# Four more up-projection chunks a layer by seven products, with weight buffers of 4 KB made further ahead

## The chip, the cores and the metric

The kernel runs on one core of one Trainium2 chip. The metric is the device time of one execution in microseconds (us), and lower is better. TensorE (PE) multiplies, VectorE (DVE) and ScalarE (ACT) do the elementwise work, GpSimd (POOL) issues the accumulating DMAs and a few small operations, and SyncE (SP) issues the loads. PEld is TensorE's loading of stationary operands, which overlaps its multiplying.

## What is computed

An encoder of two residual layers over 512 tokens of 1024 features, in float32. Layer 0 mixes tokens by a gated linear attention (GLA) in two directions, layer 1 by grouped-query softmax attention. Each layer ends with a gated MLP whose up-projection gives 2 x 2816 features, a value half and a gate half:

```python
def conv_ffn(h, w_up, w_conv, b_conv, w_down):
    u = h @ w_up
    u = lax.conv_general_dilated(
        u, w_conv[:, None, :], window_strides=(1,), padding=[(1, 1)],
        dimension_numbers=('NWC', 'WIO', 'NWC'), feature_group_count=u.shape[-1]) + b_conv
    val, gate = jnp.split(u, 2, axis=-1)
    return (jax.nn.silu(gate) * val) @ w_down
...
for i in range(DEPTH):
    h = rmsnorm(x, norm_mix[i])
    ...
    x = x + conv_ffn(rmsnorm(x, norm_ffn[i]), ffn_w_up[i], ffn_w_conv[i],
                     ffn_b_conv[i], ffn_w_down[i])
```

## The kernel before

**Layout and precision.** Activations lie with features on the 128 partitions and the 512 tokens along the free axis; x is eight tiles of 128x512. Every float32 operand of a large product is split into a high part (rounded to fp32r by ACT) and a low part (the rest, by DVE), and a product is three matmuls: high x high, high x low, low x high (mm3, L359 to L363).

**Order of the program.** GLA, MLP of layer 0, attention, MLP of layer 1. The build puts the instructions of each engine into one fixed order, which need not be that of the source; an engine runs its own in that order.

**Weights.** The class Weights (L115 to L221) keeps a list `todo` of pieces in the order of use. Weights come in strips of 1 MB (8 KB a partition); a plain strip has two pieces of 4 KB. make() (L129) loads a strip into one of two `raw` buffers of 8 KB and splits a piece into `wh` (L204, ACT) and `wl` (L205, DVE), with three buffers of 4 KB for each. Some strips named in `by_dma` are split without DVE: ACT writes the high part (L144) and the negated high part (L145), and an accumulating DMA that POOL issues (L194, in flush()) adds the raw weights to the latter. piece() hands out a piece and makes others until `ahead` of them are ready: one ahead for plain pieces, three for those of a seven-product strip.

**The MLP** (ffn, L774) has 22 chunks of 128 value and 128 gate features. A plain chunk (plain_up, L785) is two tiles `up` of 128x512 with 24 matmuls each; DVE multiplies each by the tokens' factors (L803). A chunk named in SEVEN (seven_up, L824) is computed by a seven-product scheme on 2x2 blocks, as Strassen's: features in pairs of 128, tokens in two halves of 256. Its inputs are combined once a layer, during chunks 0 to 3 (prepare_input, L899). Its weights are four quarters a21, a11, a12, a22, from which summed() (L151) makes four pieces: h=0 holds a21+a11 and a11, h=1 a21+a22 and a11+a21+a22 (into the 8 KB tile `ring`), h=2 a12 and a22 (low part by DMA), h=3 the sum for product 3 (in `sq` tiles). Each product is 12 matmuls of 128x256 (L815). Results grow in PSUM banks r1 to r5 (tags acc with three banks, s and pt with two each); ACT copies partial results between banks (L831, L835, and L846, L847, L850 at the end), DVE combines them (L840, L848 to L854). The first product of a chunk is started within the chunk before it (begin_up).

After either form, act_up (L857) does the convolution (ACT L864, DVE L865 and L866), silu (L868) and the gate (L869); after each second chunk prepare() (L878) makes the combined operands of the down-projection (L875, L876 and small ones). After chunks 9 and 17, down_part (L921) does four strips of the down-projection by the same seven products, ACT copying at L935, L944 and L950, DVE adding into x (L951, L958 to L962). The last six chunks' part of the down-projection is plain (48 units of three matmuls, `dn`), the first 16 of which need only chunks 16 to 19.

Before the change SEVEN holds chunks 5, 11, 14, 18, 19 and 21, so a layer has 16 plain chunks, 6 by seven products, and 8 strips of the down-projection by seven products. The products of a chunk run in the order 1, 6, 7, 2, 5, [1 of the next], 4, 3, and those of a down strip likewise.

The tile `ring` is also used in GLA for the split values (values, L636) and in attention for copies of the probabilities.

Of the kernel before, what the change touches and what calls it, by code (L numbers as in the profile page):

```python
# [14 lines left out]
P = 128  # L15
# [33 lines left out]
SEVEN = (5, 11, 14, 18, 19, 21)  # L49
# [10 lines left out]
def hybrid_encoder_kernel(  # L60
# [54 lines left out]
    class Weights:  # L115
# [3 lines left out]
        def __init__(self):  # L119
            self.todo, self.made, self.raw, self.by_dma, self.pending = [], {}, {}, [], []  # L120
            self.sums, self.last, self.fine = set(), None, []

        def add(self, src, strips=None, pieces=2):
            for i in strips or range(src.shape[0]):
                self.todo += [(src, i, h) for h in range(pieces)]
                if pieces > 2:
                    self.sums.add((id(src), i))

        def make(self, key):  # L129
            src, i, h = key  # L130
            if h == 0 and (id(src), i) not in self.raw:
                t = sp.tile([P, 4 * S], F32, tag="raw", bufs=2, name=nm("raw"))
                n = 4 if any(src is a and i < m for a, m in self.fine) else 1
                for q in range(n):
                    sl = slice(q * 4 * S // n, (q + 1) * 4 * S // n)
                    sync.dma_start(t[:, sl], src[i, :, sl])
                self.raw[id(src), i] = t
            if (id(src), i) in self.sums:
                self.made[id(src), i, h] = self.summed(self.raw[id(src), i], h)
                return  # L140
            r = self.raw[id(src), i][:, h * 2 * S : (h + 1) * 2 * S]
            hi, lo = pair("wh", 3, F32R, "wh"), pair("wl", 3, F32R, "wl")
            if any(src is a and i < n for a, n in self.by_dma):
                act.activation(hi, r, AF.Copy)  # L144
                act.activation(lo, r, AF.Copy, scale=-1.0)  # L145
                self.pending.append((lo, r))
# [4 lines left out]
        def summed(self, raw, h):  # L151


            a21, a11, a12, a22 = (raw[:, n * S : (n + 1) * S] for n in range(4))
            if h == 0:
                r = tmp("t", "sum")
                with tc.issue_after(self.last.ins) if self.last else ExitStack():
                    dve.tensor_tensor(r, a21, a11, ALU.add)
                    dve.tensor_tensor(a21, a21, a22, ALU.add)
                hi, lo = pair("wh", 3, F32R, "wh"), pair("wl", 3, F32R, "wl")  # L160
                for sl, y in ((slice(0, S), r), (slice(S, 2 * S), a11)):
                    act.activation(hi[:, sl], y, AF.Copy)
                    dve.tensor_tensor(lo[:, sl], y, hi[:, sl].bitcast(F32), ALU.subtract)
                return hi, lo
            if h == 1:
                dve.tensor_tensor(a11, a21, a11, ALU.add)
                r = raw[:, : 2 * S]
            elif h == 2:
                r = raw[:, 2 * S :]
            else:  # L170
                r = tmp("sq", "sum4")
                dve.tensor_tensor(r, a11, a12, ALU.add)
                hi, lo = (sp.tile([P, S], F32R, tag="sq", bufs=3, name=nm(n)) for n in ("wh4", "wl4"))
                act.activation(hi, r, AF.Copy)
                self.last = dve.tensor_tensor(lo, r, hi.bitcast(F32), ALU.subtract)
                return hi, lo
            if h == 1:
                t = sp.tile([P, 4 * S], F32R, tag="ring", bufs=1, name=nm("ring"))
                hi, lo = t[:, : 2 * S], t[:, 2 * S :]
            else:  # L180
                hi, lo = pair("wh", 3, F32R, "wh"), pair("wl", 3, F32R, "wl")
            if h == 2:
                act.activation(hi, r, AF.Copy)
                act.activation(lo, r, AF.Copy, scale=-1.0)
                self.pending.append((lo, r))
            else:
                act.activation(hi, r, AF.Copy)
                dve.tensor_tensor(lo, r, hi.bitcast(F32), ALU.subtract)
# [8 lines left out]
        def split(self, hi, lo, r, pieces, first):  # L197
# [20 lines left out]
        def ahead(self, n):  # L218
            while self.todo and n > 0:
                self.make(self.todo.pop(0))  # L220
                n -= 1  # L221

# [28 lines left out]
    W.by_dma += [(a, 1) for a in qk_order + [w_av]] + [(w_aout, 2)]  # L251
# [6 lines left out]
    raw = [sp.tile([P, 4 * S], F32, tag="raw", bufs=2, name=f"first{i}") for i in range(2)]  # L258
    for c in range(KC):
        r = slice((c % 4) * S, (c % 4 + 1) * S)  # L260
        sync.dma_start(x[c], xT[c * P : (c + 1) * P, :])
        sync.dma_start(raw[c // 4][:, r], w_vg[c // 4, :, r])
        W.raw[id(w_vg), c // 4] = raw[c // 4]
# [175 lines left out]
    def gla(norm, nxt):  # L439
# [39 lines left out]
        rw = pair("wh", 3, F32R, "rw")  # L479
# [4 lines left out]
        graw = sp.tile([P, 4 * S], F32, tag="raw", bufs=2, name="graw")  # L484
        for i in range(4):
            sync.dma_start(graw[i * 32 : (i + 1) * 32, : 2 * S], w_gate)
        gst = big(F32R, "gst")
        act.activation(gst, graw[:, : 2 * S], AF.Copy)
        pool.tensor_tensor(gst[64:96, :], graw[64:96, : 2 * S], gst[64:96, :].bitcast(F32), ALU.subtract)
# [146 lines left out]
        def values(h):  # L636

            t = sp.tile([P, 4 * S], F32R, tag="ring", bufs=1, name=nm("vr"))
            for s in range(NT):
                r = v[s][:, h * DV : (h + 1) * DV]  # L640
                hi = t[:, s * DV : (s + 1) * DV]
                act.activation(hi, r, AF.Copy)
                dve.tensor_tensor(t[:, 2 * S + s * DV : 2 * S + (s + 1) * DV], r, hi.bitcast(F32), ALU.subtract)
            return [(t[:, s * DV : (s + 1) * DV], t[:, 2 * S + s * DV : 2 * S + (s + 1) * DV]) for s in range(NT)]
# [129 lines left out]
    def ffn(layer, norm, cw, nxt):  # L774
# [10 lines left out]
        def plain_up(m):  # L785

            pss = []
            for t in range(2):
                ps = bank("s" if t else "acc", "up")
                feature_tile(*W.half(up[layer], 2 * m + t, ahead.get((m, t), 1)), norm.hl, ps)  # L790
# [10 lines left out]
            for ps in pss:  # L801
                u = tmp("u", "u")
                dve.tensor_tensor(u, ps, norm.R, ALU.mult)  # L803
                yield u
# [19 lines left out]
        def seven_up(m):  # L824
# [28 lines left out]
            yield c  # L853
            dve.scalar_tensor_tensor(d, d, -1.0, norm.R, ALU.mult, ALU.mult)  # L854
            yield d

        def act_up(m):  # L857

            res = []
            for t, u in enumerate(begun.pop(0) if m in SEVEN else plain_up(m)):  # L860
# [6 lines left out]
                res.append(y)  # L867
# [53 lines left out]
        def down_part(part, m):  # L921
# [17 lines left out]
            for n in range(NQ):  # L939
# [7 lines left out]
                go(n, 2, r1, False)  # L947
# [3 lines left out]
                dve.tensor_tensor(c[:, :H], c[:, :H], r1, ALU.add)  # L951
                go(n, 4, r3, False)
                if n + 1 < NQ:
                    begin(n + 1)
                else:
                    begin_up(m + 1)
# [5 lines left out]
                dve.tensor_tensor(c[:, H:], c[:, H:], r2, ALU.add)  # L962

# [43 lines left out]
    def attention(norm, nxt):  # L1007
# [159 lines left out]
        ring = sp.tile([P, 4 * S], F32R, tag="ring", bufs=1, name=nm("ring"))  # L1167

        def copy(h, j):

            n = (h * NT + j) % 6
            if n < 4:
                t = ring[:, n * S : (n + 1) * S]
# [158 lines left out]
```

## Time and profile before

| what | value |
|---|---|
| median of 3 runs | 1104.43 us (1104.32 to 1105.28) |
| profiled execution | 1103.4 us, its span from first to last instruction; no other time of it is listed |
| PE / PEld / DVE / ACT / POOL busy | 1096.4 / 960.6 / 870.1 / 633.5 / 97.9 us |
| matmuls | 6212 |
| GLA, 0 to 225.7 us | 225.7 us |
| MLP of layer 0, to 574.7 us | 349.0 us |
| attention, to 749.8 us | 175.1 us |
| MLP of layer 1, to the end | 353.6 us |

Stage borders are read from the first `up` matmul of each layer and the last `dn` matmul of layer 0. A busy PE is not PE at its peak: a matmul's record runs from issue to drain, and its successors are issued meanwhile. What a matmul costs in a dense stretch is the distance between two starts, and that is read from the chain of work or the timeline. The same holds in a small way on DVE and ACT, where an instruction starts before the one ahead of it has quite ended.

### The profile page before, as it was taken

To read this page: it belongs to the slowest core of one execution; us is meant where nothing else is said; L and a number is where in the kernel's file an instruction comes from. 1 tells how busy PE (TensorE), PEld (TensorE's weight loads), DVE (VectorE), ACT (ScalarE), POOL (GpSimd) and SP (SyncE) were. 2 spreads that over 40 slices of the span, in tenths; PEclk is the share of its full clock that TensorE was granted. 3 is DMA by queue.
4 is the path that set the end of the run, shared out by engine and by line. 5 is a ranking of instruction groups with operands and counts; after the bars stand their busy time and mean duration, and the time that the engine had idled before them with its cause. 6 is when DMAs were issued, how large, how long until landed. Compare 5 with 4: busy or idle time off the path is not lost.

```text
span 1103.4 us, 16108 instructions
## 1 busy us (share of the span) xinstructions
PE 1096.4 (99%) x6212; PEld 960.6 (87%) x6212; DVE 870.1 (79%) x1441; ACT 633.5 (57%) x1034; POOL 97.9 (9%) x106
## 2 busy tenths in 40 slices
PE   9999999999999999999999999999999999999998
PEld 7888888888889988899888888788888998889987
DVE  6785775669998789987964578766999878997893
ACT  5565343446656556666664777645665655665660
POOL 0100222000000000000004343000000000000000
PEclk9999999999999999999999999999999999999999
DMA  6322222222516434364457765422151643445542
GB/s 232 134 96 89 79 100 77 77 77 80 169 45 175 129 98 140 124 173 115 140 152 182 181 178 152 163 77 81 72 166 50 167 134 97 138 129 143 145 134 77
DMA packets 33149, 136.91 MB, mean 124 GB/s; under 512 B 4016, under 2 KB 4528, under 8 KB 22704
## 3 DMA queue, kind: packets, MB, share of 16 engines
q1 hardware_dynamic: 21072, 102.16, 27.1%
q0 software_dynamic: 7104, 25.17, 11.6%
q10 hardware_dynamic: 4896, 8.55, 2.1%
q8 instruction: 49, 0.80, 0.3%
q14 instruction: 28, 0.23, 0.1%
HBM read 100.21 MB, written 2.10 MB: 93 GB/s over the span
## 4 chain that ended last, share of the span: by engine, by line
PE 92%; DVE 4%; DMA 2%; ACT 1%; issue 0%; POOL 0%; ACTq 0%; DVEq 0%; SPq 0%
PE r L815 24%; PE up L361 10%; PE up L362 10%; PE up L363 10%; PE vg L393 8%; PE op L419 8%; PE dn L363 2%; PE dn L361 2%; PE dn L362 2%; PE o L687 1%; DMA ring<-p 1%; PE av L393 1%; PE pt L1191 1%; PE A L361 1%; PE q L361 1%; PE in L620 1%
## 5 line engine op out<-in xcount | busy, mean ns | idle before, releaser
L361 PE MATMUL up<-xhl,wh 128*128 128x512 f32 x512 | 199.9, 390 | 0.0
L362 PE MATMUL up<-xhl,wh 128*128 128x512 f32 x512 | 199.5, 390 | 0.0
L363 PE MATMUL up<-xhl,wl 128*128 128x512 f32 x512 | 199.3, 389 | 0.0
L204 ACT ACTIVATE wh<-raw 128x1024 fp32r<-128x1024 f32 x108 | 114.1, 1057 | 128.8 <-PE up L362 34.0
L205 DVE TENSOR_TENSOR wl<-raw,wh 128x1024 fp32r<-128x1024 f32 x108 | 132.0, 1223 | 30.2 <-ACT wh L204 29.8
L815 PE MATMUL r<-gu,wh 128*128 128x256 f32 x640 | 116.6, 283 | 0.3 <-ACT r L950 0.3
L363 PEld LDWEIGHTS up<-xhl,wl 128*128 128x128 f32 x512 | 96.1, 188 | 20.2
L362 PEld LDWEIGHTS up<-xhl,wh 128*128 128x128 f32 x512 | 96.2, 188 | 19.2
L361 PEld LDWEIGHTS up<-xhl,wh 128*128 128x128 f32 x512 | 96.2, 188 | 19.2
L815 PEld LDWEIGHTS r<-gu,wh 128*128 128x128 f32 x640 | 99.7, 191 | 0.8 <-ACT r L950 0.5
L194 POOL DMA_DIRECT2D wl<-raw x44 | 38.9, 883 | 675.5 <-ACT r L935 195.3
L864 ACT ACTIVATE y<-u,cw 128x512 f32<-128x512 f32 x88 | 68.9, 809 | 47.4 <-DVE u L803 27.1
L815 PE MATMUL r<-gu,wl 128*128 128x256 f32 x320 | 90.4, 283 | 0.0
L393 PE MATMUL vg<-wh,xhl 128*128 128x512 f32 x256 | 80.5, 394 | 0.2 <-DVE wh L202 0.2
L865 DVE SCALAR_TENSOR_TENSOR y<-u,cw,y 128x511 f32<-128x511 f32 x88 | 64.4, 750 | 12.0 <-ACT y L864 12.0
L419 PE MATMUL op<-oT,wh 128*128 128x512 f32 x256 | 71.8, 394 | 0.6 <-ACT p L1155 0.6
L866 DVE SCALAR_TENSOR_TENSOR y<-u,cw,y 128x511 f32<-128x511 f32 x88 | 64.0, 748 | 0.5
L815 PEld LDWEIGHTS r<-gu,wl 128*128 128x128 f32 x320 | 61.1, 191 | 0.0
L393 PEld LDWEIGHTS vg<-wh,xhl 128*128 128x128 f32 x256 | 48.5, 190 | 10.5 <-ACT sq L335 0.5
L419 PEld LDWEIGHTS op<-oT,wh 128*128 128x128 f32 x256 | 47.3, 188 | 11.0 <-ACT p L1155 0.9
L815 PE MATMUL r<-xhl,wh 128*128 128x256 f32 x288 | 53.3, 283 | 0.0
L815 PE MATMUL r<-gu,ring 128*128 128x256 f32 x384 | 50.8, 281 | 0.0
(264 smaller groups left out, 2475.7 us busy)
## 6 DMA issues: line engine op xcount, KB each, us to landing
raw<-in_w_up_dram SPq DMA_DIRECT2D x42, 1024.0 KB, 4.8
wl<-raw POOLq DMA_DIRECT2D x44, 512.0 KB, 4.6
raw<-in_w_down_dram SPq DMA_DIRECT2D x22, 1024.0 KB, 4.8
raw<-in_w_vg_dram SPq DMA_DIRECT2D x6, 1024.0 KB, 4.9
ring<-p ACTq DMA_DIRECT2D x22, 256.0 KB, 3.3
raw<-in_w_kq_dram SPq DMA_DIRECT2D x4, 1024.0 KB, 4.8
raw<-in_w_gout_dram SPq DMA_DIRECT2D x4, 1024.0 KB, 4.8
raw<-in_w_aout_dram SPq DMA_DIRECT2D x16, 256.0 KB, 4.2
```

What stands on the lines that cost most here:

```text
L194: pool.dma_start(lo.bitcast(F32), r, accum_op=ALU.add)
L204: act.activation(hi[:, sl], r[:, sl], AF.Copy)
L205: dve.tensor_tensor(lo[:, sl], r[:, sl], hi[:, sl].bitcast(F32), ALU.subtract)
L361: mm(ps, wh, mh, start=start, stop=False)
L362: mm(ps, wh, ml, start=False, stop=False)
L363: return mm(ps, wl, mh, start=False, stop=stop)
L393: mm(ps[j][:, :width], hl[k][i == 2][:, j * P : (j + 1) * P], (wl if i == 1 else wh)[:, sl], start=k == 0 and i == 0, stop=k == KC - 1 and ...
L419: mm(pss[ng][n], wt[:, sl], mv, start=k == 0 and i == 0, stop=k == KC - 1 and i == 2)
L815: mm(dst, w[:, sl], m, start=start and j == 0 and a == 0, stop=j == len(pairs) - 1 and a == 2, skip_group_check=True)
L864: act.activation(y, u, AF.Identity, scale=w(1), bias=w(3))
L865: dve.scalar_tensor_tensor(y[:, 1:], u[:, : S - 1], w(0), y[:, 1:], ALU.mult, ALU.add)
L866: dve.scalar_tensor_tensor(y[:, : S - 1], u[:, 1:], w(2), y[:, : S - 1], ALU.mult, ALU.add)
```

## The change

SEVEN gets chunks 7, 10, 13 and 20, so that ten chunks a layer go by seven products and twelve are plain. The order of the products is changed: 1, 6, 7, 5, 3, 4, [1 of the next], 2 in the up-projection, and 1, 6, 7, 5, 4, 3, [1 of the next], 2 in the down-projection. Pieces of an up strip are made in the order 0, 1, 3, 2. Weight memory is regrouped: four `raw`, four `wh` and four `wl` buffers of 4 KB each stand in place of two `raw` of 8 KB, three `wh`, three `wl` and the 8 KB `ring`; the total stays at 48 KB a partition. Plain up pieces are made three ahead, seven-product pieces four ahead, and the raw data of the next three pieces are loaded beyond that. Up strips 0 to 4 of each layer get their low parts by the accumulating DMA. What used `ring` now takes a `wh` and a `wl` buffer.

```diff
-SEVEN = (5, 11, 14, 18, 19, 21)
+SEVEN = (5, 7, 10, 11, 13, 14, 18, 19, 20, 21)
+UPA = 3
+PA = 4
+BYD = 5
+LOADS = 3
+NR, NH, NL = 4, 4, 4
...
+                order = (0, 1, 3, 2) if pieces > 2 and src.shape[0] == FC else range(pieces)
+                self.todo += [(src, i, h) for h in order]
...
+        def fetch(self, src, i, h):
+            key = (id(src), i, h)
+            if key in self.loaded:
+                return self.loaded.pop(key)
+            t = pair("raw", NR, F32, "raw")
+            n = 2 if any(src is a and i < m for a, m in self.fine) else 1
+            for q in range(n):
+                w = 2 * S // n
+                sync.dma_start(t[:, q * w : (q + 1) * w], src[i, :, h * 2 * S + q * w : h * 2 * S + (q + 1) * w])
+            return t
+
+        def load(self, key):
+            src, i, h = key
+            if (id(src), i) in self.sums:
+                if (id(src), i) not in self.strip:
+                    self.strip[id(src), i] = [self.fetch(src, i, 0), self.fetch(src, i, 1)]
+            else:
+                k = (id(src), i, h)
+                if k not in self.loaded:
+                    self.loaded[k] = self.fetch(*key)
...
-            hi, lo = pair("wh", 3, F32R, "wh"), pair("wl", 3, F32R, "wl")
+            hi, lo = self.two()
...
+        def two(self):
+            return pair("wh", NH, F32R, "wh"), pair("wl", NL, F32R, "wl")
+
+        def low_dma(self, hi, lo, r):
+            act.activation(hi, r, AF.Copy)
+            act.activation(lo, r, AF.Copy, scale=-1.0)
+            self.pending.append((lo, r))
...
             if h == 1:
                 dve.tensor_tensor(a11, a21, a11, ALU.add)
-                r = raw[:, : 2 * S]
+                hi, lo = self.two()
+                self.split(hi, lo, t1)
+                return hi, lo
...
-            if h == 1:
-                t = sp.tile([P, 4 * S], F32R, tag="ring", bufs=1, name=nm("ring"))
-                hi, lo = t[:, : 2 * S], t[:, 2 * S :]
...
             while self.todo and n > 0:
                 self.make(self.todo.pop(0))
                 n -= 1
+            for key in self.todo[:LOADS]:
+                self.load(key)
...
-    W.by_dma += [(a, 1) for a in qk_order + [w_av]] + [(w_aout, 2)]
+    W.by_dma += [(a, 1) for a in qk_order + [w_av]] + [(w_aout, 2)] + [(up[i], BYD) for i in range(2)]
...
         def values(h):
-            t = sp.tile([P, 4 * S], F32R, tag="ring", bufs=1, name=nm("vr"))
+            th, tl = pair("wh", NH, F32R, "vrh"), pair("wl", NL, F32R, "vrl")
...
-                feature_tile(*W.half(up[layer], 2 * m + t, ahead.get((m, t), 1)), norm.hl, ps)
+                feature_tile(*W.half(up[layer], 2 * m + t, max(UPA, ahead.get((m, t), 1))), norm.hl, ps)
...
-                pieces[h] = W.piece(src, strip, h, 3)
+                pieces[h] = W.piece(src, strip, h, PA)
...
             go(7, r4, True)
-            go(2, r1, False)
-            c, d = tmp("u", "u"), tmp("u", "u")
-            dve.tensor_tensor(c[:, :H], r1, norm.R[:, :H], ALU.mult)
             go(5, r2, False)
-            begin_up(m + 1)
-            go(4, r3, False)
             r5 = bank("pt", "r5")[:, :H]
             go(3, r5, True)
+            c, d = tmp("u", "u"), tmp("u", "u")
             act.activation(d[:, :H], r4, AF.Copy)
             act.activation(d[:, H:], r4, AF.Copy)
             dve.tensor_tensor(d[:, H:], d[:, H:], r2, ALU.add)
-            dve.tensor_tensor(d[:, :H], d[:, :H], r3, ALU.add)
             act.activation(c[:, H:], r5, AF.Copy)
             dve.tensor_tensor(c[:, H:], c[:, H:], r2, ALU.add)
             dve.tensor_tensor(c[:, H:], c[:, H:], norm.R[:, H:], ALU.mult)
-            yield c
+            go(4, r3, False)
+            begin_up(m + 1)
+            go(2, r1, False)
+            dve.tensor_tensor(d[:, :H], d[:, :H], r3, ALU.add)
             dve.scalar_tensor_tensor(d, d, -1.0, norm.R, ALU.mult, ALU.mult)
-            yield d
+            yield 1, d
+            dve.tensor_tensor(c[:, :H], r1, norm.R[:, :H], ALU.mult)
+            yield 0, c
...
                 go(n, 7, r4, True)
-                go(n, 2, r1, False)
                 go(n, 5, r2, False)
                 r5 = tmp("u", "r5", H)
                 act.activation(r5, r2, AF.Copy)
-                dve.tensor_tensor(c[:, :H], c[:, :H], r1, ALU.add)
                 go(n, 4, r3, False)
-                if n + 1 < NQ:
-                    begin(n + 1)
-                else:
-                    begin_up(m + 1)
...
                 go(n, 3, r2, False)
                 dve.tensor_tensor(c[:, H:], c[:, H:], r2, ALU.add)
+                if n + 1 < NQ:
+                    begin(n + 1)
+                else:
+                    begin_up(m + 1)
+                go(n, 2, r1, False)
+                dve.tensor_tensor(c[:, :H], c[:, :H], r1, ALU.add)
...
-        ring = sp.tile([P, 4 * S], F32R, tag="ring", bufs=1, name=nm("ring"))
+        ring = [pair(*a, F32R, "ring") for a in (("wh", NH), ("wl", NL))]
```

More of the change, by code (lines that the diff above doesn't have):

```diff
@@ L149, in make, with summed @@
             self.made[id(src), i, h] = (hi, lo)
[L151 to L154 removed]
+        def two(self):
[4 more added lines that the diff above has]
+            self.pending.append((lo, r))
+        def summed(self, src, i, h):
+            t1, t3 = self.strip[id(src), i][:2]
+            a21, a11, a12, a22 = t1[:, :S], t1[:, S:], t3[:, :S], t3[:, S:]
             if h == 0:
@@ L195, in flush, with split @@
             self.pending = []
-        def split(self, hi, lo, r, pieces, first):
+        def split(self, hi, lo, r, pieces=1, first=False):
             n = 2 * S // pieces
```

80 lines of the change are left out of this document (32 added, 48 removed).

## The prediction

> **What bounds the kernel now.** I read the page first, then PE's waits, the four stages, and the chain of work for what one matmul costs.
>
> ```profile
> span 1103.4 us, 16108 instructions
> PE 1096.4 (99%) x6212; PEld 960.6 (87%) x6212; DVE 870.1 (79%) x1441; ACT 633.5 (57%) x1034; POOL 97.9 (9%) x106
> PEclk9999999999999999999999999999999999999999
> PE 92%; DVE 4%; DMA 2%; ACT 1%; issue 0%; POOL 0%; ACTq 0%; DVEq 0%; SPq 0%
> PE warm L277 <- DVE bd L283: 1.3, 1, 1.3
> PE r L815 <- ACT r L950: 0.3, 1, 0.3
> 225.70:574.70 349.00, 349.00 (x2102) 313.03 (x2101) 302.85 (x493) 211.46 (x321) 15.05 (x17) 1.00 0.42 123
> 574.70:749.80 175.10, 173.62 (x906) 144.73 (x905) 115.95 (x217) 109.42 (x210) 43.48 (x36) 1.00 0.56 156
> 749.80:1103.40 353.60, 349.62 (x2101) 312.89 (x2099) 295.83 (x482) 200.36 (x303) 13.14 (x15) 1.00 0.39 117
> ...
> 722.75 27.20 PE op L419 x120
> 854.30 1.43 PE r L815 x12
> 912.86 8.61 PE r L815 x72
> 987.46 58.74 PE r L815 x492
> ```
>
> The three window rows are the MLP of layer 0, attention and the MLP of layer 1: length, then PE, PEld, DVE and ACT busy, clock, DMA share. PE is the chain; its clock is full; of its waits the first shown is at the start of the kernel, and the second, 0.3 us, is the only one in an MLP. A busy share of 99% could still hide slow issue, so the last four rows matter. 120 matmuls of 512 columns take 27.20 us, 0.2267 each, and 492 of 256 columns 58.74 us, 0.1194 each. An MLP has 768 + 144 of the first and 1176 of the second: 206.7 + 140.4 = 347.1 us, and some 1.4 for the norm's small matmuls (an estimate: 12 of them and their switching) make 348.5. Layer 0's stage is 349.0 long; layer 1's has 349.6 of PE work and 4.0 without, nearly all of it the tail behind the last matmul. So **PE issues without a gap in both MLPs**, and what the MLP costs is its matmuls.
>
> DVE is second: 302.9 of 349.0 and 295.8 of 353.6, 87% and 84%. The prices below are its steps in the chain, where it is followed at full speed, and ACT's mean durations in layer 1's MLP.
>
> ```profile
> 775.37 1.13 DVE wl L205
> 783.22 0.33 DVE q L890
> 783.55 0.60 DVE u L803
> 787.15 1.32 DVE y L865 x2
> 807.69 1.14 DVE ring L188
> L204 ACT ACTIVATE wh<-raw 128x1024 fp32r<-128x1024 f32 x37 | 39.1, 1057 | 36.1 <-PE up L362 16.7 <-PE dn L362 7.0 <-PE op L419 4.8
> L184 ACT ACTIVATE wl<-raw 128x1024 fp32r<-128x1024 f32 x14 | 14.6, 1044 | 0.0
> L831 ACT ACTIVATE r<-r 128x256 f32<-128x256 f32 x6 | 2.2, 366 | 1.2 <-PE r L815 1.2
> L162 ACT ACTIVATE wh<-sum 128x512 fp32r<-128x512 f32 x14 | 8.8, 628 | 0.8
> ```
>
> On DVE, 1024 columns cost 1.13 us, 512 cost 0.60, a three-operand 512 cost 0.66, 256 cost 0.33.
>
> **The change, part by part.**
>
> *PE.* A plain chunk is 48 x 0.2267 = 10.88 us; by seven products it is 84 x 0.1194 = 10.03. Each conversion removes 0.85 us; four a layer, eight in all: **-6.8 us**, on the path since PE is gapless. The reordered products are the same matmuls and cost PE nothing by themselves.
>
> [...]
>
> *DVE.* A converted chunk drops two L205 and two L803 (3.46 us) and gains seven 512-column steps (L158, L159, L163 twice, L166, L172, L175) and L188, 5.33, then L840, L848, L849, L851, L852 and L854, 2.31: 7.64 in all, +4.2 us. Four a layer are +16.7. The accumulating DMA takes the low parts of strips 0 to 4, ten times 1.13 = -11.3. Net +5.4 us: about 87% of some 347 us. As a stage this fits; locally it need not. With convolution (4 x 0.66), gate (0.60) and half a prepare() (1.73), a plain chunk holds 8.4 us of DVE work against 10.88 of PE, a seven-product chunk 12.6 against 10.03, a seven-product down strip about 7.3 against 10.03. Two sevens in a row are new in chunks 10, 11 and 13, 14, and 18 to 21 are now four. Chunks 10 to 14 give PE 4 x 10.03 + 10.88 = 51.0 us. In them DVE makes the weights of 11 to 14 (3 x 5.33 + 2.26) and three plain pieces (3.4), and finishes 10 to 13 (3 x 7.28 + 6.17): 49.7. But with its buffers full it can't work ahead in chunk 10, where some 2.6 us go unused, and prepare() falls on the odd chunks; I expect it 3 to 4 us behind at the end of 14, and level again by 17. In 18 to 21, where one split (0.60) a chunk replaces prepare(), it has 11.5 against 10.03, and is some 3 us behind at the end. Does such a lag stop PE? Rows of chunk 5 and its neighbours:
>
> ```profile
> 259.60:270.50 10.90, 10.90 (x50) 9.03 (x49) 10.90 (x20) 7.17 (x13) 0.00 (x0) 1.00 0.27 96
> 283.10:291.70 8.60, 8.60 (x74) 8.60 (x73) 8.59 (x16) 5.46 (x9) 0.00 (x0) 1.00 0.55 165
> 291.19 0.40 PE L815 MATMUL r<-xhl,wh 128*128 128x256 f32 x2
> 296.72 0.42 DVE L852 TENSOR_TENSOR u<-u,R 128x256 f32<-128x256 f32 x1
> ```
>
> DVE was full for two chunks, finished chunk 5's last combination 5 us after its last product, and PE never stood. A lag of 4 to 5 us is thus covered by the PSUM banks and weights in hand. Beyond that it costs one for one.
>
> *ACT.* A conversion adds three weight steps of 0.63 and three of 1.05 (5.0), five copies of 0.37 (1.85), and drops two L204 (2.1): +4.8 us; ten negated copies add 10.4: +30 a layer, from 200 to 230 of 347. In a run of sevens that is about 9.5 of 10.03, so ACT is nearly full there as well.
>
> *Further ahead, four buffers.* A make three ahead waits until PE has finished the piece just before, and this wait stands at the head of ACT's order; behind it are L864 of the convolution, and the copies r that PE itself waits for. In the trace such a wait cost PE once:
>
> ```profile
> 897.18 0.63 ACT L162 ACTIVATE wh<-raw 128x512 fp32r<-128x512 f32 x1 [3.43 <-DMA raw<-in_w_up_dram]
> 898.36 0.37 ACT L950 ACTIVATE r<-r 128x256 f32<-128x256 f32 x1
> 898.78 0.51 PE L815 MATMUL r<-gu,wh 128*128 128x256 f32 x2 [0.34 <-ACT r L950]
> ...
> ACT wh L204 <- PE up L362: 34.0, 25, 5.4
> L194 POOL DMA_DIRECT2D wl<-raw x44 | 38.9, 883 | 675.5 <-ACT r L935 195.3
> raw<-in_w_up_dram SPq DMA_DIRECT2D x42, 1024.0 KB, 4.8
> wl<-raw POOLq DMA_DIRECT2D x44, 512.0 KB, 4.6
> ```
>
> ACT stood 3.43 us for a late load, the copy behind it was late, and PE lost 0.34. With 4 KB buffers freed one by one, the loads start earlier; no row shows a 512 KB load, but it lies between the rows of 256 KB (3.8 us for w_up) and of 1024 KB (4.8), and I take 4.8, hidden in a buffer's cycle of some 22 us (four pieces of 5.4 us). The 25 waits for PE up to 5.4 us each cost PE nothing.
>
> [...]
>
> *Low parts by DMA.* Two ACT copies (2.1 us), the issue (0.88) and the landing (4.6) make 7.6 us from a free buffer; the piece is wanted three pieces or 16 us later, so nothing shows. POOL's order holds besides only one norm step in an MLP. Without that cover it would cost at most 7.6 - 5.4 = 2.2 us a piece.
>
> *ring gone.* Piece h=1 could be made only after product 5 and was wanted three products later (4.3 us). Now it is made from the end of product 7 and wanted five later (7.2 us), which is a relief. In GLA and attention `ring`'s users take a wh and a wl, which leaves three of each, as before. I take 0, from -1.5 to +1.5 us, as attention has 1.5 us without PE work (175.1 - 173.6).
>
> *Order of the products.* In the down strips L950 now has one product (1.43 us) instead of two between its cause, product 5, and product 3, which waits for it. How late can it be?
>
> ```profile
> 493.95 0.37 ACT L944 ACTIVATE r<-r 128x256 f32<-128x256 f32 x1 [0.85 <-PE r L815]
> 498.29 1.06 ACT L187 ACTIVATE ring<-raw 128x1024 fp32r<-128x1024 f32 x1 [0.42 <-ACT gu L875]
> 499.26 0.37 ACT L950 ACTIVATE r<-r 128x256 f32<-128x256 f32 x1
> 1058.57 8.61 PE r L815 x72
> 1076.14 0.69 DVE L876 TENSOR_TENSOR gu<-y,gu 128x512 fp32r<-128x512 f32 x1 [0.70 <-ACT gu L875]
> ```
>
> L944 starts with product 6's end; three products later, at about 498.2, product 5 ended, and L950 came 1.0 us after that, behind L187. It would have ended at 499.6, just as a single product ends: 0 to 0.2 us of stall a strip, 0 to 3.2 us for 16, and I take 0.4. In both forms r2's next copy needs DVE's last use of r2; it has two products (2.9 us). At the end of the MLP, chunk 21's operands are wanted 16 x 3 x 0.2267 = 10.9 us after its last product. Before, in layer 1, that product ended at 1067.2, the need came at 1078.1, and the last split (L876 at 1076.14) left 1.2 us to spare; now the gate half starts one product earlier, but DVE may be 3 us late: 0 to 2 us a layer, I take 0.3.
>
> *Sum.* -6.8, +0.4 (L950), +0.6 (two ends), and -0.4 for layer 1's own hold-ups (its stall of 0.34 at 898.78): **-6.2 us**, so 1097.2 against the span of 1103.4. The median of the runs shown is 1.0 above that span: **1098.2 us**.
>
> **The rivals.**
>
> *A. DVE and ACT take part of it.* If their lag passes the cover by 1 to 2.5 us at 14 and at 21 in each layer, 2 to 5 us come back: 1100.2 to 1103.4. For: both engines are over 95% full in the runs of sevens. Against: the rows of chunk 5.
>
> *B. Slower: the order on ACT.* If makes at the head of ACT's order hold up the copies that PE waits for, as at 898.78, in each seven-product strip, 16 + 20 = 36 places lose 0.34 us: 12.2 - 6.8 gives 1104.4 + 5.4 = 1109.8. It decides from 6.8 / 36 = 0.19 us a place. For: more makes, longer ahead, ACT fuller. Against: one such stall in 28 strips before, and that from a load.
>
> *C. It doesn't do what it says.* If the 256-column matmuls of the new chunks start 0.1295 us apart (10.88 / 84) and not 0.1194, the gain is nil: 1104.4. The row of 492 in a stretch, over four strips and two up chunks, speaks against it.
>
> *D. More gain.* Earlier loads take attention's 1.5 us without PE work and as much in GLA, 1 to 3 us in all: 1095.2 to 1097. No row names a load as their cause.
>
> **How the numbers follow.** Forecast (1097 to 1100.2) 0.56; A 0.20; B 0.12; C 0.03; D 0.09. Runs of this kernel lie within about 0.1% of each other, and some 0.2%, 2.2 us, is what a measurement can tell from no change: 1102.2 to 1106.6. Faster takes the forecast, D and most of A, 0.81; same the rest of A, C and the near edge of B, 0.08; slower the rest of B, 0.11. The range reaches from D's lower end to A's upper: 1095.2 to 1103.4.
>
> **What would show it.** L361, L362 and L363 each go from 512 to 384 matmuls of `up`, L815 from 2352 to 3024, still 0.119 us apart in stretches of sevens; POOL issues 44 + 20 + 8 = 72 low parts (L194). Each MLP some 3 us shorter. DVE near 10 of 10 in chunks 10 to 14 and 18 to 21 with PE waits in the MLPs under 1 us. Waits of PE for `r` copies (L935, L944, L950 and their likes) of over 3 us would show B; PE waiting for `wl` or for a `u` step, A. It would be wrong if either MLP grew, or if PE's distances in the new chunks were above 0.125 us.

## The result and the profile after

The changed kernel takes 1114.64 us (median of 4 runs, 1113.38 to 1115.93), the kernel before 1104.83 beside it: a ratio of 1.0087, with a 95% interval of 1.0072 to 1.0101. It is slower by 9.8 us where 6.2 less were forecast, and outside the range.

In the rows of the changed kernel the lines stand some 20 lower in the file: the products' matmuls are L837, a plain tile's L383 to L385, the split on ACT and DVE L223 and L224, the two ACT copies of a low part by DMA L175 and L176, their accumulating DMA L213, the copies r2 and r3 of a seven-product chunk L853 and L857. From the page, the rows that answer to those of before: span, busy times, the chain by engine, the matmuls on low parts of a down strip, one of a plain tile, and the low parts' landing.

```profile
span 1114.1 us, 17221 instructions
PE 1097.2 (98%) x6500; PEld 973.9 (87%) x6500; DVE 880.4 (79%) x1501; ACT 681.1 (61%) x1126; POOL 122.3 (11%) x134
PE 88%; DMA 5%; DVE 4%; issue 3%; ACT 1%; DVEq 0%; SPq 0%; ACTq 0%; POOLq 0%
L837 PE MATMUL r<-gu,wl 128*128 128x256 f32 x448 | 127.8, 285 | 6.5 <-DMA wl<-raw 6.5
L383 PE MATMUL up<-xhl,wh 128*128 128x512 f32 x384 | 150.0, 391 | 0.0
wl<-raw POOLq DMA_DIRECT2D x72, 512.0 KB, 5.2
```

PE's share of the chain fell from 92% to 88%, and DMA and "issue" took its place. The stages say where, by the same borders as before (MLP of layer 0, attention, MLP of layer 1 with the tail; length, then PE, PEld, DVE, ACT and POOL busy, clock, DMA share, GB/s):

```profile
227.70:581.50 353.80, 349.22 (x2246) 318.62 (x2245) 311.15 (x525) 233.29 (x365) 25.27 (x29) 1.00 0.53 142
581.50:755.90 174.40, 172.97 (x906) 145.20 (x905) 113.26 (x215) 112.10 (x212) 44.81 (x38) 1.00 0.58 158
755.90:1114.10 358.20, 349.86 (x2245) 319.66 (x2243) 303.15 (x514) 220.19 (x345) 22.62 (x26) 1.00 0.50 133
```

Each MLP grew, by 4.8 and 4.6 us. GLA is 2.0 longer, but e2 to e12 below, whose GLA is the same, have it between 225.4 and 227.9, so that is scatter from run to run. To see what the MLPs lost I added up, over all matmuls of an MLP, how far two starts lie apart beyond the dense distance, 0.2267 us (512 columns) or 0.1194 us (256). Called "lost" here, this is 0.2 + 1.1 us in the two MLPs before, and 7.9 + 8.7 after, in steps of over 25 ns; smaller steps add 2.0 against 0.9. So -6.8 of matmuls, +15.2 lost and +1.2 of small steps make +9.6, beside the +9.4 that the stages show. The matmuls were saved; PE's unbroken run was not.

PE's waits name the releaser (us in total, times, longest):

```profile
PE r L837 <- DMA wl<-raw: 6.7, 5, 2.3
PE r L837 <- ACT r L853: 1.9, 2, 1.0
```

The largest is the **low part of piece h=2 of a down strip**, made by the accumulating DMA. Four of these waits stand at one place: product 4 of the second strip of each down part. By the starts they cost 1.5 to 2.5 us each, some 0.2 more than the idle time listed. The chain of work through the first of them, from the last `up` matmul on:

```profile
338.43 4.33 PE r L837 x36
...
342.79 3.97 issue
346.77 7.62 DMA wl<-raw
...
354.43 5.66 PE r L837 x45
```

and the instructions at that place, from the timelines of ACT, POOL, SP and PE:

```profile
343.52 1.06 ACT L223 ACTIVATE wh<-raw 128x1024 fp32r<-128x1024 f32 x1 [0.24 <-DVE raw L195]
344.49 1.04 ACT L175 ACTIVATE wh<-raw 128x1024 fp32r<-128x1024 f32 x1
345.44 1.04 ACT L176 ACTIVATE wl<-raw 128x1024 fp32r<-128x1024 f32 x1
346.77 0.86 POOL L213 DMA_DIRECT2D wl<-raw  x1 [11.56 <-ACT wl L176]
339.56 15.21 SPq L144 DMA_DIRECT2D raw<-in_w_down_dram  x3
354.43 0.39 PE L837 MATMUL r<-gu,wl 128*128 128x256 f32 x1 [1.38 <-DMA wl<-raw]
```

Read it from the top. The chain takes its start at product 5 of the first strip, which ended at 342.79; then come piece h=1's copy (L223, which stands ahead of h=2 in ACT's order and waits for DVE's sum), h=2's own two copies, and the issue: 3.97 us. The landing takes 7.62 us, not the 4.6 of the row of before, while SP's loads of the next strips run beside it. That makes 11.6 us, and seven products of 1.43, or 10.0, pass on PE meanwhile. The 1.6 us between the two is the wait. The other three places have the same times on ACT within 0.1 us: h=2's first copy starts 1.9 us behind the end of product 5.

In the kernel before, ACT took the two pieces the other way round. From its timeline, at a down part of layer 1 (L183 and L184 are h=2's two copies, L187 is h=1's):

```profile
874.08 1.06 ACT L183 ACTIVATE wh<-raw 128x1024 fp32r<-128x1024 f32 x1 [0.29 <-PE r L815]
875.05 1.04 ACT L184 ACTIVATE wl<-raw 128x1024 fp32r<-128x1024 f32 x1
877.05 1.06 ACT L187 ACTIVATE ring<-raw 128x1024 fp32r<-128x1024 f32 x1 [0.96 <-PE r L815]
```

There h=2 was taken up as product 7 ended, and h=1, which had to wait for `ring`, came behind it.

### The profile page after: what moved, and what is told of

The parts are those of the page before. It is cut to its first block, busy times and chain, and to the rows that moved or that the text cites. A ratio compares the mean times of both kernels' runs of the same rounds, so it can differ in the third digit from the quotient of the medians.

```text
span 1114.1 us, 17221 instructions
## 1 busy us (share of the span) xinstructions
PE 1097.2 (98%) x6500; PEld 973.9 (87%) x6500; DVE 880.4 (79%) x1501; ACT 681.1 (61%) x1126; POOL 122.3 (11%) x134
## 4 chain that ended last, share of the span: by engine, by line
PE 88%; DMA 5%; DVE 4%; issue 3%; ACT 1%; DVEq 0%; SPq 0%; ACTq 0%; POOLq 0%
PE r L837 26%; PE vg L415 8%; PE op L441 8%; PE up L383 7%; PE up L384 7%; PE up L385 7%; DMA wl<-raw 4%; PE dn L383 2%; PE dn L384 2%; PE dn L385 2%; PE av L415 1%; PE o L709 1%; PE A L383 1%; PE B L383 1%; PE A L385 1%
## 5 line engine op out<-in xcount | busy, mean ns | idle before, releaser
L223 ACT ACTIVATE wh<-raw 128x1024 fp32r<-128x1024 f32 x108 | 114.0, 1055 | 93.7 <-DVE raw L195 20.1
L837 PE MATMUL r<-gu,wh 128*128 128x256 f32 x896 | 164.4, 285 | 0.0
L224 DVE TENSOR_TENSOR wl<-raw,wh 128x1024 fp32r<-128x1024 f32 x108 | 132.3, 1226 | 24.9 <-ACT wh L223 24.4
L383 PE MATMUL up<-xhl,wh 128*128 128x512 f32 x384 | 150.0, 391 | 0.0
L384 PE MATMUL up<-xhl,wh 128*128 128x512 f32 x384 | 149.6, 390 | 0.0
L385 PE MATMUL up<-xhl,wl 128*128 128x512 f32 x384 | 149.4, 389 | 0.0
L213 POOL DMA_DIRECT2D wl<-raw x72 | 62.6, 869 | 759.2 <-ACT wl L176 507.6
L837 PEld LDWEIGHTS r<-gu,wh 128*128 128x128 f32 x896 | 141.3, 193 | 1.5
L837 PE MATMUL r<-gu,wl 128*128 128x256 f32 x448 | 127.8, 285 | 6.5 <-DMA wl<-raw 6.5
L837 PE MATMUL r<-xt,wh 128*128 128x256 f32 x640 | 118.1, 284 | 2.1 <-ACT r L853 1.9
L837 PEld LDWEIGHTS r<-xt,wh 128*128 128x128 f32 x640 | 99.9, 191 | 3.6 <-ACT r L853 2.3
L175 ACT ACTIVATE wh<-raw 128x1024 fp32r<-128x1024 f32 x72 | 75.9, 1054 | 44.2 <-PE op L441 13.8
L837 PEld LDWEIGHTS r<-gu,wl 128*128 128x128 f32 x448 | 86.6, 193 | 7.3 <-DMA wl<-raw 7.3
L837 PE MATMUL r<-xt,wl 128*128 128x256 f32 x320 | 90.7, 283 | 0.3 <-DMA wl<-raw 0.2
L837 PE MATMUL r<-xhl,wh 128*128 128x256 f32 x480 | 88.9, 283 | 0.0
L385 PEld LDWEIGHTS up<-xhl,wl 128*128 128x128 f32 x384 | 72.1, 188 | 15.1
L384 PEld LDWEIGHTS up<-xhl,wh 128*128 128x128 f32 x384 | 72.2, 188 | 14.3
L383 PEld LDWEIGHTS up<-xhl,wh 128*128 128x128 f32 x384 | 72.1, 188 | 14.3
L837 PEld LDWEIGHTS r<-xhl,wh 128*128 128x128 f32 x480 | 75.4, 192 | 0.5
L176 ACT ACTIVATE wl<-raw 128x1024 fp32r<-128x1024 f32 x72 | 75.3, 1046 | 0.2 <-PE op L441 0.2
```

The lines of the kernel that those rows point to most:

```text
L213: pool.dma_start(lo.bitcast(F32), r, accum_op=ALU.add)
L223: act.activation(hi[:, sl], r[:, sl], AF.Copy)
L224: dve.tensor_tensor(lo[:, sl], r[:, sl], hi[:, sl].bitcast(F32), ALU.subtract)
L383: mm(ps, wh, mh, start=start, stop=False)
L384: mm(ps, wh, ml, start=False, stop=False)
L385: return mm(ps, wl, mh, start=False, stop=stop)
```

## The experiments

Three theories stood at first. **Theory 1:** piece h=2 of the down strips comes late, by its buffer, by its place behind h=1 on ACT, and by the landing. **Theory 2:** the new order of products leaves the r copies too little time. **Theory 3:** DVE and ACT are too full with ten seven-product chunks (rival A of the prediction). The kernel before took 1105.01, 1104.72, 1105.51 and 1106.27 us beside e1 to e4, e5 to e8, e9 to e11 and e12.

**e1: the conversions alone.** The kernel before with only this:

```diff
-SEVEN = (5, 11, 14, 18, 19, 21)
+SEVEN = (5, 7, 10, 11, 13, 14, 18, 19, 20, 21)
```

> The kernel before with the ten chunks of the changed kernel in SEVEN, and nothing else of the change. Theory 1 (the low part of piece h=2 lands too late for product 4, because of when its buffers come free in the new grouping): here the buffers and the order of products are the old ones, so the eight conversions show their 6.8 us, less 0 to 3 us of DVE lag: 1098 to 1101 us. Theory 2 (the new order of products delays the copies that PE waits for): the same 1098 to 1101. Theory 3 (VectorE and ScalarE are full with ten chunks by seven products): the loss comes here too, 1108 to 1115.

Measured: 1113.21 us, ratio 1.0071 (1.0056 to 1.0086). A miss for theories 1 and 2, which had the loss in the new buffers or orders; it lies where theory 3 had it. With the old ones the ten chunks lose 9.8 + 8.1 us as well, at other places than the changed kernel. Its waits and, from ACT's timeline, one place (L831 is the r copy; L183, L184 and L187 make weights, L875 an operand):

```profile
PE r L815 <- ACT r L831: 3.7, 2, 1.9
PE up L363 <- DVE wl L205: 2.7, 2, 1.6
PE r L815 <- DMA wl<-raw: 2.3, 2, 1.9
...
534.55 1.05 ACT L183 ACTIVATE wh<-raw 128x1024 fp32r<-128x1024 f32 x1
535.50 0.62 ACT L875 ACTIVATE gu<-y 128x512 fp32r<-128x512 f32 x1
536.01 1.05 ACT L184 ACTIVATE wl<-raw 128x1024 fp32r<-128x1024 f32 x1
536.96 1.05 ACT L187 ACTIVATE ring<-raw 128x1024 fp32r<-128x1024 f32 x1
537.91 0.37 ACT L831 ACTIVATE r<-r 128x256 f32<-128x256 f32 x1
```

ACT runs these four back to back, and the copy that PE needs stands behind them, 3.36 us after the first one's start. Converted chunks alone, in the old buffers and orders, cost 8 us.

**e2: everything but the conversions.** The changed kernel with `SEVEN = (5, 11, 14, 18, 19, 21)`.

> The changed kernel with the six old chunks in SEVEN: buffers, order, making ahead and low parts by DMA stay. Theory 1: the four long waits in the down strips (1.5 to 2.6 us each, some 7.5 in all) and the 2 us of GLA stay: 1112 to 1117 us. Theory 2: the 16 down strips keep most of the loss: 1111 to 1116. Theory 3: the loss is gone: 1103 to 1106.

Measured: 1116.05 us, ratio 1.0096 (1.0081 to 1.0112). The four waits of the down strips stand without any converted chunk, as theory 1 has it; by theory 3 the loss would have gone:

```profile
PE r L837 <- DMA wl<-raw: 5.9, 4, 2.0
```

Each half of the change costs by itself: 8 us the conversions, 11 the rest, and both together 10. So neither theory 1 nor theory 3 holds alone, and the two costs don't add up.

**e3: no late DMA in the down strips.** The changed kernel, with h=2 of the down strips split by ACT and DVE:

```diff
                 hi, lo = self.two()
-                self.low_dma(hi, lo, t3)
+                if src.shape[0] == FC:
+                    self.low_dma(hi, lo, t3)
+                else:
+                    self.split(hi, lo, t3)
```

> The changed kernel, but in the 16 down strips the low part of piece h=2 is a subtraction on VectorE in place of the negated copy and the accumulating DMA. Theory 1: the four long waits in the down strips go, 7 us and perhaps the slow clock behind one of them (1.6), while VectorE takes 1.13 us a strip more where it has 2.7 to spare: 1104 to 1108 us. Theory 2 and theory 3: no gain, 1114 to 1117, or worse for VectorE's 18 us of added work.

Measured: 1107.59 us, ratio 1.0024 (1.0014 to 1.0034): 7 us of the 9.8 are gone, and with them all four waits for a DMA. DVE had room for the eight subtractions a layer (PE's waits for it in the MLPs stay at one of 0.5 us, as in the changed kernel), so its load was not what failed there.

**e4: the old order of products and pieces** in the new buffers: up 1, 6, 7, 2, 5, 4, 3 and down likewise, pieces made in the order 0, 1, 2, 3.

> The changed kernel with the old order of products (1, 6, 7, 2, 5, [1 of the next], 4, 3), in up chunks and down strips, and pieces made in the order 0, 1, 2, 3. Theory 1: in the new grouping piece h=2 gets its buffer from product 5 of the strip before, and product 2 wants it 5 products (7.2 us) later, not 7: every strip waits, 1118 to 1130 us. Theory 2: the loss goes, 1098 to 1104. Theory 3: no change, 1113 to 1116.

Measured: 1144.04 us, ratio 1.0356 (1.0334 to 1.0378), with

```profile
PE r L837 <- DMA wl<-raw: 23.0, 14, 4.0
PE r L837 <- ACT r L853: 7.2, 4, 2.7
```

Theory 2 falls: the new order wants h=2 later and eases the wait that it was blamed for. The time is even above theory 1's 1118 to 1130; several of the waits are followed by a stretch at a granted clock near half (a row at the end has 0.54 over 3.4 us).

**e5: piece 2 ahead of piece 1.** The changed kernel with one line different:

```diff
-                order = (0, 1, 3, 2) if pieces > 2 and src.shape[0] == FC else range(pieces)
+                order = ((0, 1, 3, 2) if src.shape[0] == FC else (0, 2, 1, 3)) if pieces > 2 else range(pieces)
```

> The changed kernel with the pieces of a down strip made in the order 0, 2, 1, 3, so that the piece whose low part comes by the accumulating DMA is made before the one that VectorE splits. Theory 1 (the low part of piece 2 is late because its buffer comes free late and ACT serves piece 1 first): piece 2 now takes the buffer that comes free one product earlier, and is ahead in ACT's order, so the four waits of 1.5 to 2.5 us at the fourth product of the second strips go or fall below 0.5 us, and the half-clock stretch behind one of them goes too; but piece 1, wanted three products in, gets the later buffer and ACT's later place, so a wait of up to 1 us on ACT or VectorE can stand there: 1106 to 1110. Theory 3 (ACT and VectorE are full): the wait only moves to piece 1, whose copy and subtraction now come last, 1113 to 1117.

Measured: 1105.34 us, ratio 1.0007 (0.9998 to 1.0017), a little below the range given: the order in which a down strip's pieces are made is worth some 9 us (1.0087 against 1.0007). The wait did not move to piece 1. From POOL's timeline and PE's waits:

```profile
341.44 0.86 POOL L213 DMA_DIRECT2D wl<-raw  x1 [12.81 <-DVE raw L195]
...
PE r L837 <- ACT r L853: 2.0, 2, 1.0
PE r L837 <- DMA wl<-raw: 0.2, 1, 0.2
```

The DMA is issued 3.2 us earlier than in the changed kernel, counted from the first `up` of the layer (341.44 - 225.6 against 346.77 - 227.7). ACT's timelines divide this: h=2's buffer comes free one product (1.4 us) earlier, with product 7, and ACT takes h=2 up 0.1 us after that, where it was 1.9 behind h=1 and DVE's sum. The DMA also lands faster: the same low part takes 6.18, 4.60, 4.54 and 4.55 us in the four down parts, where the changed kernel has 7.62, 7.26, 8.56 and 7.64. What is left is chunk 11, where from ACT's timeline

```profile
417.68 1.04 ACT L175 ACTIVATE wh<-raw 128x1024 fp32r<-128x1024 f32 x1
418.63 0.61 ACT L206 ACTIVATE wh<-sum 128x512 fp32r<-128x512 f32 x1
419.15 1.04 ACT L176 ACTIVATE wl<-raw 128x1024 fp32r<-128x1024 f32 x1
420.10 1.04 ACT L223 ACTIVATE wh<-raw 128x1024 fp32r<-128x1024 f32 x1
421.04 0.36 ACT L853 ACTIVATE r<-r 128x256 f32<-128x256 f32 x1
```

the r copy again stands behind weights, and PE is 1.26 us late.

**e6: no plain up piece by DMA.** The changed kernel with `BYD = 0`.

> The changed kernel with no plain up piece on the low-part DMA (the first five strips of each layer go back to VectorE's subtraction): 40 landings fewer of 512 KB in all, 20 VectorE subtractions more, 20 ACT copies and 20 GpSimd issues fewer. Theory 1 with the lateness set by buffers and order alone: the four waits of the down strips and those of chunk 11 stand as they were, 1113 to 1116. Were the traffic of the first strips a cause of the long landings, the four waits would shrink and the time fall by 2 us or more. Theory 3 (VectorE is full): waits on VectorE appear in chunks 5 and 7, 1115 to 1118.

Measured: 1111.44 us, ratio 1.0051 (1.0034 to 1.0067), 3 us better than the changed kernel: a miss for the first view, by which the waits would stand. The gain is that of the second view, but its reason does not fit, as the next lines show. The second strip of the first down part no longer waits (its low part landed in 5.18 us); the third does, by 0.5 us (7.43 us), and the others are 1.85, 0.80 and 1.53. In layer 1 a new wait of 1.6 us stands at 835.21, for an r3 copy (L857) behind weights and operands on ACT. The strips 0 to 4 were done long before, so their transfers can't have run beside these. The landing of 5.18 us cost no wait, that of 7.43 cost 0.5. The loads beside them run at other times than in the changed kernel (on SP's timelines from 333.88 to 351.95 us here, from 339.56 to 354.77 there); how BYD shifts them was not settled.

**e7: chunk 16 for chunk 10**, on e3: `SEVEN = (5, 7, 11, 13, 14, 16, 18, 19, 20, 21)`.

> The kernel of e3 (VectorE makes the low part of piece 2 of the down strips) with chunk 16 converted in place of chunk 10, so that no seven-product chunk stands directly ahead of chunk 11, behind the first down part. If what is left in e3 at chunk 11 (2.3 us in the first MLP, 1.5 in the second) comes from two conversions one behind the other there, it goes: 1103 to 1105, level with the kernel before. If the waits only move to chunks 14 to 18, 1107 to 1109.

Measured: 1113.99 us, ratio 1.0081 (1.0062 to 1.0101). A miss, and an instructive one. Chunk 11 is free of waits, as foreseen, but each layer now waits 3.2 us in the second down part, at the second strip's r2 (L960 in this file), where DVE is late and ACT's copy with it. The granted clock is 0.50 there besides, from 481.1 to 484.5 and from 1006.8 to 1013.5 us:

```profile
PE r L840 <- ACT r L960: 6.2, 2, 3.1
...
474.26 2.00 ACT L226 ACTIVATE wh<-raw 128x1024 fp32r<-128x1024 f32 x2 [1.71 <-DVE raw L195]
479.35 0.37 ACT L960 ACTIVATE r<-r 128x256 f32<-128x256 f32 x1 [2.04 <-DVE x L981]
```

This is theory 3, at one place: the seven-product chunk just ahead of the second down part left DVE behind as that part began, and PE waited 3.2 us in each layer.

**e8: the six old chunks with e3's mending.**

> The kernel of e2 (the new buffers and orders with the six old seven-product chunks) with VectorE making the low part of piece 2 of the down strips. Theory 1: that late piece is the whole cost of the regrouping; 6.6 us of waits and two stretches at half clock go from e2's 1116.0, so 1105 to 1107, level with the kernel before. If the new buffers and orders cost by themselves (ACT and VectorE, the order of products), only the 7 us go that e3 gained on the changed kernel: 1108 to 1110.

Measured: 1108.96 us, ratio 1.0033 (1.0020 to 1.0046), which is what the second view expected, though PE lost only 2.1 + 1.6 us in the MLPs. With this mending, four conversions a layer (e3 against e8, 1.0024 against 1.0033) gain some 1 us, and the two intervals overlap; e3 still loses 5.9 + 4.3 us in the MLPs, 3.8 of it at chunk 11.

**e9, e11, e12: where the seven-product chunks stand**, all on e5; **e10** is e5 with the six old ones.

```diff
-SEVEN = (5, 7, 10, 11, 13, 14, 18, 19, 20, 21)
+SEVEN = (5, 7, 11, 12, 13, 14, 18, 19, 20, 21)   # e9
+SEVEN = (5, 7, 11, 13, 14, 15, 18, 19, 20, 21)   # e11
+SEVEN = (5, 7, 11, 13, 14, 18, 19, 20, 21)       # e12
```

> The kernel of e5 (pieces of a down strip in the order 0, 2, 1, 3) with chunk 12 converted in place of chunk 10. What is left in e5 stands mostly at chunk 11 (2.1 us in the first MLP, 2.2 in the second), where ACT runs four conversions of weight pieces ahead of a product copy, because chunk 10's seven products follow straight on the down part. If that place is the cause, it goes, and the conversions' gain comes through: 1105.3 - 4.3 = 1101, 1100 to 1103, faster than the kernel before. If four seven-product chunks in a row fill ACT and VectorE, the waits move to chunks 12 to 14: 1104 to 1107.

> The kernel of e5 with the six old seven-product chunks. Beside e9 it gives what the four conversions a layer are worth where no piece is late: 8 x 0.85 = 6.8 us by the count of matmuls, so 1107 to 1109 if e9 is at 1101. Were the new buffers and orders free by themselves, it would stand at the kernel before, 1105; e8 stood 2 to 4 us above that with only 2 us of waits left that are long enough to be named.

> As e9, with chunk 15 in place of chunk 10, so that three seven-product chunks stand in a row and two plain ones come before the next down part's products. As e9 if only the neighbourhood of chunks 10 and 11 mattered: 1100 to 1103. If a seven-product chunk near the second down part holds ACT back there, as chunk 16 did in e7 (3.2 us a layer), 1104 to 1108.

> The kernel of e5 with nine seven-product chunks a layer: chunk 10 is plain and nothing takes its place. The matmuls cost 2 x 0.85 = 1.7 us more than in e5, and the waits of chunk 11 (4.3 us in both MLPs) go; beside e11 the third seven-product chunk in a row goes, with its waits of 3.9 us: 1101 to 1103. If waits of that kind belong to the number of conversions and not to their places, it stands at 1104 or above.

| kernel | us | ratio to before | lost in the MLPs, us |
|---|---|---|---|
| e5: ten, with 10 | 1105.34 | 1.0007 (0.9998 to 1.0017) | 4.0 + 3.4 |
| e9: ten, 12 for 10 | 1107.65 | 1.0022 (1.0014 to 1.0031) | 5.1 + 4.7 |
| e10: six | 1108.09 | 1.0022 (1.0012 to 1.0032) | 1.2 + 0.7 |
| e11: ten, 15 for 10 | 1103.59 | 0.9981 (0.9972 to 0.9990) | 3.3 + 2.5 |
| e12: nine, none for 10 | 1102.44 | 0.9965 (0.9951 to 0.9979) | 1.5 + 1.2 |

e9 missed its first view: in chunks 11 to 14, four in a row, PE waits for piece h=3, the sum for product 3,

```profile
PE r L837 <- ACT wh L206: 3.1, 2, 1.5
PE r L837 <- DVE wl L207: 2.4, 2, 1.2
```

Chunks 18 to 21, four in a row in most of these kernels, have no such waits (e5 lists none in its MLPs), so the number in a row is not all of it. e11, with three in a row, loses less and beats the kernel before; e12 drops one conversion, pays 1.7 us more matmuls, has no PE wait over 0.32 us in either MLP, and is the best, 0.35% faster than before. Its two MLPs, with the columns of the windows above:

```profile
227.90:576.30 348.40, 348.25 (x2210) 317.19 (x2209) 307.04 (x515) 228.49 (x356) 24.42 (x28) 1.00 0.52 143
...
749.70:1101.50 351.80, 348.27 (x2209) 316.98 (x2207) 298.81 (x504) 215.09 (x336) 21.77 (x25) 1.00 0.48 134
```

The MLPs of e12 take 696.5 us (without the tail of 3.7), those of e10 700.5: 4.0 less for six conversions, whose matmuls are 5.1 us less, with 0.9 more lost. With the 0.9 added back that is 0.82 us a conversion, near the 0.85 of the sum: the price holds where no piece is late.

What stays open: e10, with the six old chunks and almost no waits, is 2.4 us (ratio 1.0012 to 1.0032) above the kernel before. In its profiled run the MLPs are 1.6 us longer than those of before, 1.0 of it in steps of under 25 ns, and attention is 2.0 longer. There PE waited 2.4 us for a DMA (`ring<-p`), which others of these kernels have at 0.3 to 2.0 us, and from 708.7 to 712.1 the granted clock was 0.50. The record suggests that this stretch is most of the excess: the three runs of e10 with a granted clock of 1.0 took 1105.63 to 1107.22 us, the other eight, at 0.998 or 0.999, 1107.95 to 1110.86. Where the clock fell in the runs without a profile is not known.

## Why the prediction was wrong

*What bounds the kernel* was right: PE, without gaps, so that any wait shows in full. That held against the forecast too: -6.8 of matmuls, +15.2 lost and +1.2 of small steps come to +9.6 us where the MLPs grew by 9.4.

*PE's -6.8 us* was right. The counts came as foreseen (384 `up` matmuls on each of L383 to L385, 72 low parts on POOL), and e12 against e10 gives the price, 0.82 us a chunk against 0.85.

*Low parts by DMA* is **the step that failed**. It summed 2.1 + 0.88 + 4.6 to 7.6 us from a free buffer and set that against three pieces or 16 us, "so nothing shows". That fits the plain up pieces. The pieces that stopped PE were those which already went by DMA and whose timing the change moved: h=2 of the down strips. There the way is 3.97 us to the issue, h=1's copy and a DVE sum among it, plus a landing of 7.6; the need comes seven products or 10.0 us after. Both terms were mis-sized: nothing was counted for h=1 ahead on ACT, and the landing was taken at its median, 4.6 us, where the four took 7.26 to 8.56. e3 (no DMA) takes 7 us back, e5 (h=2 first) some 9, of the 16 between forecast and result. In e5 the -6.8 of the matmuls is made up by 6.1 us more lost than before (4.4 stand at chunk 11) and 1.2 of small steps. Such small steps are 1.9 to 2.2 in the kernels with the new buffers and orders and 0.8 in e1; what makes them was not separated. No run gives h=2 the earlier buffer without the earlier place; by the timelines of e5 the buffer is 1.4 us of its 3.2 and ACT's order 1.8.

*ring gone* looked at h=1 alone and called it a relief. It was one for h=1; but h=1 then took the wh and wl that h=2 had used, and h=2 got those of one piece later. ACT's order turned with it: before, `ring` held h=1 back behind h=2 (874.08 to 877.05 above); freed from it, h=1 went first and held h=2 back. The step followed the piece that the diff moves, not the next to draw on the same buffers and the same engine. e5 gives ACT its old order of the two again. GLA and attention bore out the 0 taken for them, within their scatter.

*DVE and ACT, "a lag of 4 to 5 us is thus covered"*: that came from one pair of chunks and does not hold everywhere; that a lag beyond it costs one for one was an estimate, which no run tests alone. e1, e7 and e9 lose 1 to 3 us at single places where ACT or DVE come late with weights or r copies, and the changed kernel 1.0 + 0.9 us at chunk 11. The latter is rival B's mechanism (weights at the head of ACT's order ahead of a copy that PE needs), but at a few places for 1 to 3 us each, not at 36 for 0.34; and in e7, with DVE behind, it is rival A's. B's 1109.8 was on the right side by luck, as it held nothing of the DMA. The sign given for rival A, PE waiting for `wl`, came too, but most of those waits are for the DMA and not for DVE, which had room in e3. Two sums of this part were off: DVE grew by 8.3 and 7.3 us a layer, not 5.4, and ACT by 21.8 and 19.8, not 30, in part since mean durations were added up, and instructions overlap (in ACT's rows at 343.52 by 0.09 us).

*Order of the products*: for L950, 0.4 us was taken from 0 to 3.2. Eight down strips of the changed kernel have a step of 0.17 us, 1.4 us if all are this copy's (L971 in the new file), and none has more beside the four waits. e4 shows what the new order is worth in these buffers: 29 us.

*The two ends and attention's earlier loads* changed nothing that can be seen. The 4.8 us taken for a 512 KB load rested on the reading that no row shows one; the kernel before has one (`rope`, 5.7 us). In the changed kernel such loads took 3.8 us (w_up) and 4.3 (w_down), so nothing hung on it.

## What to carry to other kernels

When buffers are regrouped, follow every piece that draws on the group, not only the one that was moved: when its buffer comes free, what stands ahead of it on the engine that fills it, and how long its slowest landing takes (9.02 us in the changed kernel, where the page's median is 5.2), against the time until it is wanted. On an engine with a fixed order, make first the piece with the longest way to its consumer: that took the changed kernel from 1114.64 us to the 1105.34 of e5. And where PE ran without gaps here, a conversion was worth its matmuls only at a place where the engines that feed it were not already behind: nine chunks (e12, 1102.44 us) did better than the ten of e5 and e9 (1105.34 and 1107.65), and the lead over the best ten (e11, 1103.59) is within the intervals.

## What the runs showed of the hardware

**A wait of 2.47 us was followed by 1.6 us of further loss.** Behind PE's wait of that length at 880.52 in the changed kernel, the granted clock is 0.50 for 3.41 us, from 883.68 to 887.09, and some 1.6 us more are lost: the matmuls of 256 columns start 0.214 us apart there and not 0.1194. The window row just behind it (columns as above; the clock stands before the DMA share), then two of e4, behind waits of 1.96 and 1.94 us, then one of e6, behind 1.85:

```profile
883.10:886.60 3.50, 3.48 (x18) 3.48 (x19) 0.42 (x1) 0.00 (x0) 0.86 (x1) 0.58 0.62 150
```

```profile
488.40:491.80 3.40, 3.39 (x28) 3.40 (x29) 1.81 (x3) 0.66 (x2) 0.00 (x0) 1.00 0.58 175
520.70:524.10 3.40, 3.40 (x17) 3.40 (x18) 1.07 (x2) 0.73 (x3) 0.00 (x0) 0.54 0.48 154
```

```profile
480.50:483.90 3.40, 3.36 (x28) 3.37 (x29) 0.84 (x2) 1.04 (x2) 0.86 (x1) 1.00 0.68 199
```

In the traces of this study no wait in an MLP of up to 1.85 us was followed by such a stretch, and 12 of the 15 from 1.94 us on were; those of 1.96 and 2.90 us in e4 and one of 2.04 in e1 were not. Where the ends of a stretch are given, it is 3.4 us long here, in e10 and at 481.1 in e7, and 6.7 at 1006.8 in e7. What sets the clock, and why the waits of 1.94 and 1.96 us in e4 differ, was not shown.

**The accumulating DMAs that ran beside loads had the longer landings.** In the changed kernel the 8 low parts that no load of SP overlaps land in 4.55 to 5.20 us, the 64 that one does in 4.49 to 9.02, median 5.33. Before, 23 of 44 were alone and took 4.49 to 6.74, median 4.56, and the other 21 took 4.52 to 8.72, median 4.78; that one of 6.74 shows that loads are not the only cause, and no run changed the loads alone. The medians of the page's DMA rows, 4.6 before and 5.2 after, don't show the landings that PE met at the four waits, 7.26 to 8.56.
